# A 128-byte spare tile behind the constants' pool, and two steps of a two-layer hybrid decoder issued two ticks later

## The chip, the cores and the metric

One Trainium2 chip, one NeuronCore of it. The metric is the device time of one execution in microseconds (us), the median of three. Engines are named as in the profile: PE is TensorE (PEld its weight loads), DVE VectorE, ACT ScalarE, POOL GpSimd, SP SyncE.

## What is computed

Two layers of a decoder trunk on x of 512 tokens by 1024 channels, float32:

```python
for l in range(2):
    x = x + 0.5 * swiglu(rms_norm(x, ffn1_norm[l]), ffn1_w_up[l], ffn1_w_down[l])   # hidden 2816
    h = rms_norm(x, mix_norm[l])
    q, k, v, z, xbc, dt_raw, gate_sb, gate_ssm = split(h @ w_in[l])
    y_sb = stick_breaking_attention(q, k, v) @ w_branch_sb[l]                       # 4 heads of 128
    xbc = silu(causal_depthwise_conv(xbc, conv_w, conv_b))                          # 4 taps
    y_ssm = mamba2_ssd(z, xbc, dt_raw, ...) @ w_branch_ssm[l]                       # 24 heads of 64, 8 groups
    x = x + (sigmoid(gate_sb) * y_sb + sigmoid(gate_ssm) * y_ssm) @ w_out[l]
    x = x + 0.5 * swiglu(rms_norm(x, ffn2_norm[l]), ffn2_w_up[l], ffn2_w_down[l])
return rms_norm(x, final_norm)
```

## The kernel before

x is kept transposed, as 8 blocks of 128 channels by 512 tokens. Every large product is done at nearly fp32 precision with three fp32r matmuls, `mm3` (L313): high part by high part (L315 in the trace), high by low (L316) and low by high (L317). A weight unit (128x1024) is read from HBM into `wraw`, cast on ACT into `whi` (L282) and its remainder taken on DVE into `wlo` (L284, `convert`). Activations are split alike: `hhi`/`hlo` hold a normed or scaled block, `th`/`tl` differences of two half blocks, `act` the FFN's hidden blocks, `yt` the mixer's transposed tiles (q, k, later the SSM's output), `ohi`/`olo` the attention's output.

The FFN's up product works on 2x2 blocks with seven products in place of eight (`pair_of_blocks`, L576): matmuls of 256 columns, four of seven products with `th`/`tl` as the operand that streams and three with `hhi`/`hlo`. Most others stream 512 columns.

**Order of work.** The engines run what the program text issues, in order. After each `mm3` of a long product `dense` (L320) calls `tick()` (L208), which moves every side generator on whose count has run out; `yield n` in a generator means "go on n ticks later", so n ticks stand for n times three matmuls on PE. The generators that matter here:

- `norm_end` (L522): sums the squares of x over channels. ACT casts the sum `acc` to `rs` (L527), DVE takes the remainder `sq` (L529), PE sums both over the partitions with two matmuls by `nones` (L533), ACT computes an estimate of the reciprocal root (L537 to L539), DVE refines it (L541 to L543). It is spawned six times: at the opening, behind the first FFN of each layer (for the mixer's norm), behind each mixer, and behind the first layer's second FFN. In the FFN and the opening, products start on blocks that are not yet normed, and are scaled by `rs` afterwards; in the mixer the first three products do so, then DVE scales the eight blocks of x in place (`scale_blocks`, L363) and splits them again (`swapped`, L355), since the later products take normed blocks.
- `conv_block` (L1017): the four taps of the causal convolution on DVE (L1028, three instructions), tanh on ACT (L1033), the product that ends silu on DVE (L1040, into `cv`, `bT` or `cT`), then for the x and b blocks four (b: three) transposes on PE (`transposed`, L854) into a `pt` bank of PSUM, and a copy of them on ACT. x and b blocks of the 8 groups feed the groups' SSD steps.
- `mixer` (L1268) holds one loop that waits, while the program is being issued, until four blocks are scaled.

**Where tiles lie.** Pools that open on the left of SBUF follow one another from the pool of the constants, `cst`, on: constants, norm tiles, `hhi`/`hlo`, `wraw`, `whi`/`wlo`, `act`, the mixer's left pools. x, `uv`/`th`/`tl`, `yt` and `ohi`/`olo` are in pools on the right, laid out from the far end. In each partition the left tiles named here begin 96 bytes behind a multiple of 256, the right ones 224 behind one: left and right stand 128 bytes apart, counted within 256.

Of the kernel before, what the change touches and what calls it, by code (L numbers as in the profile page):

```python
# [8 lines left out]
F32 = mybir.dt.float32  # L9
# [8 lines left out]
P = 128  # L18
# [67 lines left out]
def conv_at(kind, i):  # L86

    if kind == "x":
        return OFF_X + i * P, i * TAPS
    at = (OFF_B, OFF_C)[kind == "c"] + i * P  # L90
    return at, (DIN // P + GROUPS * (kind == "c") + i) * TAPS
# [72 lines left out]
class Builder:  # L164
# [357 lines left out]
    def norm_end(self, wait):  # L522

        nc = self.nc
        yield wait - 2
        two = [self.t(self.nrm, [P, SEQ], tag, F32R) for tag in ("rs", "sq")]
        nc.scalar.copy(two[0], self.acc)  # L527
        yield 2
        nc.vector.tensor_tensor(two[1], self.acc, two[0].bitcast(F32), op=ALU.subtract)  # L529
        yield 2  # L530
        ps = self.t(self.ptr, [P, SEQ], "pt")
        for part in two:
            nc.tensor.matmul(ps, self.nones, part, start=part is two[0], stop=part is two[1])  # L533
        yield 3
        y, t = self.t(self.nrm, [P, SEQ], "rs"), self.t(self.nrm, [P, SEQ], "acc")
        v = self.t(self.nrm, [P, SEQ], "sq")
        nc.scalar.activation(y, ps, AF.Ln, scale=-1.0 / DM, bias=self.eps)  # L537
        nc.scalar.activation(y, y, AF.Exp, scale=-0.5)
        nc.scalar.activation(v, ps, AF.Identity, scale=-1.0 / DM, bias=self.eps)  # L539
        yield 3  # L540
        nc.vector.tensor_tensor(t, y, v, op=ALU.mult)  # L541
        nc.vector.scalar_tensor_tensor(t, t, -0.5, y, op0=ALU.mult, op1=ALU.mult)
        nc.vector.scalar_tensor_tensor(y, t, 1.5, y, op0=ALU.add, op1=ALU.mult)  # L543
        self.rs = y
# [472 lines left out]
    def conv_block(self, kind, i, ps):  # L1017


        nc, mp = self.nc, self.mp  # L1020
        r = yield from self.take("raw")
        u = yield from self.take("cv")
        _, k0 = conv_at(kind, i)
        tap = [self.conv[:, k0 + j:k0 + j + 1] for j in range(TAPS)]
        nc.scalar.activation(u, ps, AF.Identity, scale=tap[KCONV - 1], bias=tap[KCONV])
        yield 2
        for j in range(1, KCONV):
            nc.vector.scalar_tensor_tensor(u[:, j:], ps[:, :SEQ - j], tap[KCONV - 1 - j], u[:, j:],  # L1028
                                           op0=ALU.mult, op1=ALU.add)
            yield 1  # L1030
        yield 1
        yield from self.opened()
        nc.scalar.activation(r, u, AF.Tanh)  # L1033
        yield 1
        if self.cumb is None:
            self.load_cum(0)
        dst = u
        if kind != "x":
            dst = self.ssm[i][kind] = self.t(mp, [P, SEQ], kind + "T")
        nc.vector.scalar_tensor_tensor(dst, r, 1.0, u, op0=ALU.add, op1=ALU.mult)  # L1040
        yield 3
        if kind == "x":
            p, i = divmod(i, 3)
            pt = self.transposed(dst)
            yield 1
            for g in (2 * p, 2 * p + 1):
                a, b = max(i * P, g % 2 * GW), min((i + 1) * P, (g % 2 + 1) * GW)
                if a < b:
                    if "x" not in self.ssm[g]:
                        while not self.room["xs"]:  # L1050
                            yield 1
                        self.room["xs"] -= 1
                        self.ssm[g]["x"] = self.t(mp, [P, NT, GW], "xs", bufs=3)
                    nc.scalar.activation(self.ssm[g]["x"][:, :, a - g % 2 * GW:b - g % 2 * GW],
                                         pt[:, :, a - i * P:b - i * P], AF.Copy, scale=0.5)
                    self.ssm[g]["x", i] = True
            yield 1
        elif kind == "b":
            pt = self.transposed(dst, NT - 1)
            yield 1  # L1060
            tok = self.t(mp, [P, NT - 1, P], "btok")
            nc.scalar.copy(tok, pt)
            self.ssm[i]["btok"] = tok
        self.give("raw", "cv")
# [326 lines left out]
    def build(self):  # L1391
        nc, tc, enter = self.nc, self.tc, self.ctx.enter_context
        self.cst = enter(tc.tile_pool(name="cst", bufs=1))
        self.nrm = enter(tc.tile_pool(name="nrm", bufs=1))
        self.hp = enter(tc.tile_pool(name="hp", bufs=KB))
        self.wraw = enter(tc.tile_pool(name="wraw", bufs=3))
        self.wsp = enter(tc.tile_pool(name="wsp", bufs=3))
        self.dr = enter(tc.tile_pool(name="dr", bufs=2, space=DRAM))
        self.pmm = enter(tc.tile_pool(name="pmm", bufs=4, space=PSUM))
        self.pa = enter(tc.tile_pool(name="pa", bufs=2, space=PSUM))  # L1400
        self.ptr = enter(tc.tile_pool(name="ptr", bufs=2, space=PSUM))
        self.open_x()
        self.open_t()
        self.tt = [self.t(self.tp, [P, SEQ], "tl", bufs=KB) for _ in range(KB)]
        nc.scalar.preload_act_table_set("natural_log_exp_and_others")
        self.pars = [self.cst.tile([P, NPAR], F32, name=f"par{layer}") for layer in range(DEPTH)]
        self.opening_loads()
        self.consts()
        warm = self.t(self.ptr, [P, SEQ], "pt")
        for _ in range(8):  # L1410
            nc.tensor.matmul(warm[:, :P], self.ones, self.ones, start=True, stop=True)
        self.norm_start()
        for m in range(KB):
            self.spawn(self.norm_square(m), 16 + m)
        self.spawn(self.norm_end(30))
        for layer in range(DEPTH):
            par = self.pars[layer]
            self.ffn(layer, 1, par[:, G_FFN1:G_FFN1 + KB], par[:, G_MIX:G_MIX + KB])
            self.mixer(layer)
            if layer < DEPTH - 1:  # L1420
                self.ffn(layer, 2, par[:, G_FFN2:G_FFN2 + KB], self.pars[layer + 1][:, G_FFN1:G_FFN1 + KB])
        self.xg = [None] * KB
        self.ffn(DEPTH - 1, 2, self.pars[DEPTH - 1][:, G_FFN2:G_FFN2 + KB], None)
        self.close_t()
        self.xpool.__exit__(None, None, None)
# [107 lines left out]
```

## Time and profile before

| | |
|---|---|
| median of three runs | 2587.27 us (2586.95 to 2587.41) |
| the profiled execution | 2588.58 us, of it 2586.9 us from the first to the last instruction |
| PE busy | 2565.8 us, 99% of the span, 15028 matmuls |
| DVE, ACT, POOL busy | 1752.7 (68%), 1281.7 (50%), 499.3 us (19%) |
| granted TensorE clock | mean 0.999 of full speed |
| chain that ended last | PE 93%, DVE 4%, ACT 2% |

The profile gives busy shares over the whole span first and then the chain of work that ended last, followed back from the end. Waits of an engine are listed by line and by what ended them; the timeline gives each instruction's start and length. Matmuls are pipelined: one is listed as longer than the distance to the next one's start, so distances between starts are what PE's time is made of.

### The profile page before, as it was taken

To read this page: it belongs to the slowest core of one execution; us is meant where nothing else is said; L and a number is where in the kernel's file an instruction comes from. 1 tells how busy PE (TensorE), PEld (TensorE's weight loads), DVE (VectorE), ACT (ScalarE), POOL (GpSimd) and SP (SyncE) were. 2 spreads that over 40 slices of the span, in tenths; PEclk is the share of its full clock that TensorE was granted. 3 is DMA by queue.
4 is the path that set the end of the run, shared out by engine and by line. 5 is a ranking of instruction groups with operands and counts; after the bars stand their busy time and mean duration, and the time that the engine had idled before them with its cause. 6 is when DMAs were issued, how large, how long until landed. Compare 5 with 4: busy or idle time off the path is not lost.

```text
span 2586.9 us, 38169 instructions
## 1 busy us (share of the span) xinstructions
PE 2565.8 (99%) x15028; PEld 2289.6 (89%) x15028; DVE 1752.7 (68%) x2426; ACT 1281.7 (50%) x2103; POOL 499.3 (19%) x614
## 2 busy tenths in 40 slices
PE   9999999999999999999999999999999999999998
PEld 8898988888888889899998989888888888899997
DVE  8576875676664478586885858756666644776766
ACT  6343556655554255343653535566555533543444
POOL 0121201143341002121121312012433310022120
PEclk9999999999999999999999999999999999999999
DMA  6454442233333455545364544423333334456452
GB/s 188 132 157 138 131 138 87 99 103 110 103 107 105 132 161 140 167 139 162 108 180 139 155 143 136 136 74 109 98 106 107 111 112 135 153 141 172 140 163 78
DMA packets 104659, 335.76 MB, mean 130 GB/s; under 512 B 11872, under 2 KB 15392, under 8 KB 104480
## 3 DMA queue, kind: packets, MB, share of 16 engines
q1 hardware_dynamic: 92672, 292.84, 33.9%
q0 software_dynamic: 10944, 39.85, 8.6%
q8 instruction: 118, 1.93, 0.3%
q10 hardware_dynamic: 864, 0.64, 0.1%
q14 instruction: 61, 0.50, 0.1%
HBM read 320.60 MB, written 12.68 MB: 129 GB/s over the span
## 4 chain that ended last, share of the span: by engine, by line
PE 93%; DVE 4%; ACT 2%; issue 1%; DMA 0%; POOL 0%; DVEq 0%; SPq 0%; ACTq 0%
PE mm L315 26%; PE mm L317 25%; PE mm L316 25%; PE pa L316 3%; PE pa L317 3%; PE pa L315 3%; PE pa L1170 2%; DVE wlo L284 1%; PE pa L1172 1%; PE pt L854 1%; PE pt L1155 1%; DVE cv L1028 1%; PE pt L1153 1%; ACT whi L282 1%; PE pa L453 1%
## 5 line engine op out<-in xcount | busy, mean ns | idle before, releaser
L282 ACT CAST whi<-wraw 128x1024 fp32r<-128x1024 f32 (+3 forms) x440 | 434.8, 989 | 593.0 <-PE mm L317 492.5
L284 DVE TENSOR_TENSOR wlo<-wraw,whi 128x1024 fp32r<-128x1024 f32 (+3 forms) x440 | 538.9, 1225 | 168.8 <-ACT whi L282 167.3
L315 PE MATMUL mm<-hhi,whi 128*128 128x512 f32 (+1 forms) x1584 | 564.5, 356 | 0.0
L317 PE MATMUL mm<-hlo,whi 128*128 128x512 f32 (+1 forms) x1584 | 553.4, 349 | 0.4 <-DVE hlo L507 0.4
L316 PE MATMUL mm<-hhi,wlo 128*128 128x512 f32 (+1 forms) x1584 | 552.3, 349 | 0.0
L317 PEld LDWEIGHTS mm<-hlo,whi 128*128 128x128 f32 x1584 | 299.7, 189 | 40.4 <-DVE hlo L507 0.8
L316 PEld LDWEIGHTS mm<-hhi,wlo 128*128 128x128 f32 x1584 | 300.1, 189 | 34.4
L315 PEld LDWEIGHTS mm<-hhi,whi 128*128 128x128 f32 x1584 | 300.0, 189 | 34.4 <-ACT hhi L505 0.4
L284 DVE TENSOR_TENSOR wlo<-s,whi 128x1024 fp32r<-128x1024 f32 x152 | 235.2, 1562 | 60.3 <-ACT whi L282 60.3
L315 PE MATMUL mm<-act,whi 128*128 128x512 f32 (+1 forms) x710 | 273.9, 386 | 0.0
L317 PE MATMUL mm<-act,whi 128*128 128x512 f32 (+1 forms) x710 | 273.9, 386 | 0.0
L316 PE MATMUL mm<-act,wlo 128*128 128x512 f32 (+1 forms) x710 | 273.9, 386 | 0.0
L315 PE MATMUL mm<-th,whi 128*128 128x256 f32 x912 | 257.1, 282 | 0.0
L317 PE MATMUL mm<-tl,whi 128*128 128x256 f32 x912 | 256.7, 281 | 0.0
L316 PE MATMUL mm<-th,wlo 128*128 128x256 f32 x912 | 256.5, 281 | 0.0
L626 POOL TENSOR_TENSOR g<-g,rs 128x512 f32<-128x512 f32 x76 | 132.7, 1747 | 554.9 <-DVE g L633 536.0
L282 ACT CAST whi<-s 128x1024 fp32r<-128x1024 f32 x152 | 159.3, 1048 | 102.4 <-PE mm L317 60.7
L652 DVE SCALAR_TENSOR_TENSOR x<-mm,x 128x512 f32<-128x512 f32 x93 | 64.1, 689 | 196.0 <-PE mm L317 196.0
L254 POOL DMA_DIRECT2D s<-in_wflat_dram x76 | 65.8, 865 | 625.0 <-DMA s<-in_wflat_dram 331.3
L315 PEld LDWEIGHTS mm<-th,whi 128*128 128x128 f32 x912 | 172.1, 189 | 0.0
L316 PEld LDWEIGHTS mm<-th,wlo 128*128 128x128 f32 x912 | 171.8, 188 | 0.0
L317 PEld LDWEIGHTS mm<-tl,whi 128*128 128x128 f32 x912 | 171.7, 188 | 0.0
(306 smaller groups left out, 5094.6 us busy)
## 6 DMA issues: line engine op xcount, KB each, us to landing
wraw<-in_wflat_dram SPq DMA_DIRECT2D x328, 512.0 KB, 3.6
s<-in_wflat_dram SPq DMA_DIRECT2D x76, 512.0 KB, 4.6
s<-in_wflat_dram POOLq DMA_DIRECT2D x76, 512.0 KB, 7.4
wraw<-in_wflat_dram SPq DMA_DIRECT2D x88, 384.0 KB, 3.1
cumb<-cum_d SPq DMA_DIRECT2D x16, 768.0 KB, 4.8
xd<-x SPq DMA_DIRECT2D x16, 256.0 KB, 3.3
wraw<-in_wflat_dram SPq DMA_DIRECT2D x16, 256.0 KB, 3.3
x<-xd SPq DMA_DIRECT2D x16, 256.0 KB, 3.8
```

Of the source, the lines that this page charges most:

```text
L254: self.nc.gpsimd.dma_start(raw, src, accum_op=ALU.add)
L282: nc.scalar.copy(hi[:, :n], raw[:, :n])
L284: nc.vector.tensor_tensor(lo[:, :n], raw[:, :n], hi[:, :n].bitcast(F32), op=ALU.subtract)
L315: mm(ps, a[0], b[0], start=start, stop=False, **kw)
L316: mm(ps, a[1], b[0], start=False, stop=False, **kw)
L317: mm(ps, a[0], b[1], start=False, stop=stop, **kw)
L453: nc.tensor.matmul(p, parts[a][:, ks], h[b], start=k + a + b == 0, stop=k == KB - 1 and b == 1)
L626: eng.tensor_tensor(r, r, self.rs[:, cols].unsqueeze(1).to_broadcast([P, 2, half]), op=ALU.mult)
L652: self.nc.vector.scalar_tensor_tensor(x, pd, 0.5, x, op0=ALU.mult, op1=ALU.add)
L854: self.nc.tensor.transpose(pt[:, cs], src[:, cs], self.ident)
L1028: nc.vector.scalar_tensor_tensor(u[:, j:], ps[:, :SEQ - j], tap[KCONV - 1 - j], u[:, j:], op0=ALU.mult, op1=ALU.add)
L1170: nc.tensor.matmul(py[:, i * HD:(i + 1) * HD], decs[c][:, i, :], xdts[c][:, i, :], start=True, stop=True)
```

## The change

Three edits. `cst` gets a first tile of 32 fp32 per partition that nothing reads or writes: every left tile lies 128 bytes higher, right tiles stay. In `norm_end` the pair of matmuls and all that follows is issued two ticks later. In `conv_block` the transposes and the copies from them are issued two ticks later, and so is the return of the block's two tiles (`give`), which a later block takes.

```diff
@@ norm_end
         yield 2
         nc.vector.tensor_tensor(two[1], self.acc, two[0].bitcast(F32), op=ALU.subtract)
-        yield 2
+        yield 4
         ps = self.t(self.ptr, [P, SEQ], "pt")
@@ conv_block
         nc.vector.scalar_tensor_tensor(dst, r, 1.0, u, op0=ALU.add, op1=ALU.mult)
-        yield 3
+        yield 5
         if kind == "x":
@@ build
         self.cst = enter(tc.tile_pool(name="cst", bufs=1))
+        self.cst.tile([P, 32], F32, name="gap")
         self.nrm = enter(tc.tile_pool(name="nrm", bufs=1))
```

No instruction is added or removed on any engine. Tile names carry a running number, which the spare tile raises by one; lines behind L1394 stand one lower. Three places where the order of an engine moves:

DVE at the norm ahead of the first layer's mixer, before (`wlo` is a weight unit's low part, L541 to L543 refine the norm's root, L363 scales a block of x):

```order
L529 TENSOR_TENSOR sq_3480<-acc_3234,rs_3479 128x512
L284 TENSOR_TENSOR wlo_3489<-wraw_3403,whi_3488 128x1024
L541 TENSOR_TENSOR acc_3515<-rs_3514,sq_3516 128x512
L542 SCALAR_TENSOR_TENSOR acc_3515<-acc_3515,rs_3514 128x512
L543 SCALAR_TENSOR_TENSOR rs_3514<-acc_3515,rs_3514 128x512
L363 SCALAR_TENSOR_TENSOR x_86<-x_86,par_106,rs_3514 128x512
L363 SCALAR_TENSOR_TENSOR x_87<-x_87,par_106,rs_3514 128x512
L284 TENSOR_TENSOR wlo_3530<-wraw_3440,whi_3529 128x1024
```

The same place in the change:

```order
L529 TENSOR_TENSOR sq_3481<-acc_3235,rs_3480 128x512
L284 TENSOR_TENSOR wlo_3490<-wraw_3404,whi_3489 128x1024
L284 TENSOR_TENSOR wlo_3531<-wraw_3441,whi_3530 128x1024
L541 TENSOR_TENSOR acc_3525<-rs_3524,sq_3526 128x512
L542 SCALAR_TENSOR_TENSOR acc_3525<-acc_3525,rs_3524 128x512
L543 SCALAR_TENSOR_TENSOR rs_3524<-acc_3525,rs_3524 128x512
L363 SCALAR_TENSOR_TENSOR x_87<-x_87,par_107,rs_3524 128x512
```

The second weight remainder (`wlo_3530`, now `wlo_3531`) stands ahead of the norm's three instructions instead of behind them and two blocks of L363. On ACT the cast that feeds it stays behind L539, the last of the norm's three activations.

PE in the mixer's SSD part, first layer, one of the convolved x blocks, before (`cv` is the convolved block, `pt` the bank that takes its transposes, `raw` a group's result, which another generator transposes):

```order
L317 MATMUL mm_5907<-hlo_3589,whi_5799 128x512
L854 MATMUL pt_5925<-ident,cv_5853 128x128 x4
L315 MATMUL mm_5907<-hhi_3596,whi_5799 128x512
L316 MATMUL mm_5907<-hhi_3596,wlo_5800 128x512
L317 MATMUL mm_5907<-hlo_3597,whi_5799 128x512
L854 MATMUL pa_5935<-ident,raw_5893 128x128 x4
```

and in the change:

```order
L317 MATMUL mm_5908<-hlo_3589,whi_5792 128x512
L315 MATMUL mm_5908<-hhi_3597,whi_5792 128x512
L316 MATMUL mm_5908<-hhi_3597,wlo_5793 128x512
L317 MATMUL mm_5908<-hlo_3598,whi_5792 128x512
L315 MATMUL mm_5908<-hhi_3604,whi_5792 128x512
L316 MATMUL mm_5908<-hhi_3604,wlo_5793 128x512
L317 MATMUL mm_5908<-hlo_3605,whi_5792 128x512
L854 MATMUL pt_5935<-ident,cv_5852 128x128 x4
L315 MATMUL mm_5908<-hhi_3611,whi_5792 128x512
L316 MATMUL mm_5908<-hhi_3611,wlo_5793 128x512
L317 MATMUL mm_5908<-hlo_3612,whi_5792 128x512
L854 MATMUL pa_5944<-ident,raw_5901 128x128 x4
```

The transposes stand six matmuls of 512 columns later, and so does the work of the group around them.

DVE ahead of the transposes of the second convolved x block of the layer (`z` is the gate of the SSM), before:

```order
L1028 SCALAR_TENSOR_TENSOR cv_4819<-mm_4717,conv_4132,cv_4819 128x509
L1087 SCALAR_TENSOR_TENSOR z_4382<-raw_4853,z_4382 128x384
L1028 SCALAR_TENSOR_TENSOR cv_4857<-mm_4774,conv_4132,cv_4857 128x511
L284 TENSOR_TENSOR wlo_4860<-wraw_4718,whi_4859 128x1024
L1040 SCALAR_TENSOR_TENSOR cv_4819<-raw_4818,cv_4819 128x512
```

and in the change:

```order
L1028 SCALAR_TENSOR_TENSOR cv_4828<-mm_4718,conv_4133,cv_4828 128x509
L1028 SCALAR_TENSOR_TENSOR cv_4847<-mm_4775,conv_4133,cv_4847 128x511
L284 TENSOR_TENSOR wlo_4850<-wraw_4719,whi_4849 128x1024
L1087 SCALAR_TENSOR_TENSOR z_4370<-raw_4863,z_4370 128x384
L1028 SCALAR_TENSOR_TENSOR cv_4847<-mm_4775,conv_4133,cv_4847 128x510
L1087 SCALAR_TENSOR_TENSOR z_4383<-raw_4872,z_4383 128x384
L1028 SCALAR_TENSOR_TENSOR cv_4847<-mm_4775,conv_4133,cv_4847 128x509
L1040 SCALAR_TENSOR_TENSOR cv_4828<-raw_4827,cv_4828 128x512
```

Here PE reaches the transposes 12 matmuls later, and on DVE four more instructions (two L1087, two L1028) stand between the weight remainder and L1040.

## Rows read from the trace of the kernel before

**Rows 1.** The page: busy time of each engine, its share and instructions.

```profile
PE 2565.8 (99%) x15028; PEld 2289.6 (89%) x15028; DVE 1752.7 (68%) x2426; ACT 1281.7 (50%) x2103; POOL 499.3 (19%) x614
```

**Rows 2.** Waits of PE, by line and releaser: us in total, times, longest us.

```profile
PE pt L854 <- DVE cv L1040: 4.8, 8, 0.8
...
PE pt L533 <- DVE sq L529: 0.7, 1, 0.7
```

**Rows 3.** Timeline of PE, one site of transposes: start, us, instruction [idle before, releaser].

```profile
608.49 0.39 PE L317 MATMUL mm<-hlo,whi 128*128 128x512 f32 x1
609.41 0.66 PE L854 MATMUL pt<-ident,cv 128*128 128x128 f32 x4 [0.54 <-DVE cv L1040]
```

**Rows 4.** Timeline of DVE at the same site.

```profile
608.67 0.69 DVE L1040 SCALAR_TENSOR_TENSOR cv<-raw,cv 128x512 f32<-128x512 f32 x1 [0.16 <-ACT raw L1033]
```

**Rows 5.** Timeline of PE, the first late site of the layer.

```profile
507.35 0.39 PE L317 MATMUL mm<-hlo,whi 128*128 128x512 f32 x1
508.50 0.33 PE L854 MATMUL pt<-ident,cv 128*128 128x128 f32 x1 [0.76 <-DVE cv L1040]
```

**Rows 6.** Timeline of DVE at the first late site.

```profile
505.96 0.74 DVE L1028 SCALAR_TENSOR_TENSOR cv<-mm,conv,cv 128x511 f32<-128x511 f32 x1
506.62 1.21 DVE L284 TENSOR_TENSOR wlo<-wraw,whi 128x1024 fp32r<-128x1024 f32 x1
507.76 0.68 DVE L1040 SCALAR_TENSOR_TENSOR cv<-raw,cv 128x512 f32<-128x512 f32 x1
```

**Rows 7.** Timeline of PE, the norm behind the first layer's second FFN.

```profile
1300.07 0.39 PE L533 MATMUL pt<-rs,nones 128*128 128x512 f32 x1
1301.17 0.50 PE L533 MATMUL pt<-sq,nones 128*128 128x512 f32 x1 [0.72 <-DVE sq L529]
```

**Rows 8.** Timeline of DVE from the mixer's norm to the first tiles of q and k.

```profile
364.24 0.69 DVE L541 TENSOR_TENSOR acc<-rs,sq 128x512 f32<-128x512 f32 x1 [2.83 <-ACT sq L539]
...
367.82 1.22 DVE L284 TENSOR_TENSOR wlo<-wraw,whi 128x1024 fp32r<-128x1024 f32 x1
368.95 3.40 DVE L363 SCALAR_TENSOR_TENSOR x<-x,par,rs 128x512 f32<-128x512 f32 x5
...
381.81 1.88 DVE L408 TENSOR_TENSOR yt<-raw,yt 128x512 fp32r<-128x512 f32 x3
```

**Rows 9.** Timeline of ACT and of PE, the same stretch.

```profile
364.99 1.06 ACT L282 CAST whi<-wraw 128x1024 fp32r<-128x1024 f32 x1 [0.79 <-PE pa L317]
...
383.15 0.33 PE L316 MATMUL pa<-yt,yt 128*128 128x128 f32 x1 [0.45 <-DVE yt L408]
```

**Rows 10.** Timeline of PE, ends of runs of equal matmuls of 512 columns: `act`, then `yt`.

```profile
99.21 0.39 PE L316 MATMUL mm<-act,wlo 128*128 128x512 f32 x1
...
105.11 0.39 PE L315 MATMUL mm<-act,whi 128*128 128x512 f32 x1
...
834.56 0.39 PE L315 MATMUL mm<-yt,whi 128*128 128x512 f32 x1
...
840.86 0.40 PE L315 MATMUL mm<-ohi,whi 128*128 128x512 f32 x1
```

**Rows 11.** Timeline of PE, starts of runs of 256 columns: `th`, `hhi`, `th`, `hhi`, `th`.

```profile
999.63 0.28 PE L315 MATMUL pa<-th,whi 128*128 128x256 f32 x1
...
1005.33 0.28 PE L315 MATMUL pa<-hhi,whi 128*128 128x256 f32 x1
...
1008.19 0.28 PE L315 MATMUL mm<-th,whi 128*128 128x256 f32 x1
...
1011.04 0.28 PE L315 MATMUL mm<-hhi,whi 128*128 128x256 f32 x1
...
1016.80 0.28 PE L315 MATMUL mm<-th,whi 128*128 128x256 f32 x1
```

**Rows 12.** Groups of PE instructions by line and shape: count | busy us, mean ns.

```profile
L315 PE MATMUL mm<-th,whi 128*128 128x256 f32 x912 | 257.1, 282 | 0.0
...
L315 PE MATMUL mm<-yt,whi 128*128 128x512 f32 x192 | 75.8, 395 | 0.0
```

## The prediction

> **What bounds the kernel.** I read the busy times first: PE is busy for 99% of the span, with DVE next at 68% [rows 1]. Only two things can move the end, then: the few places where PE waits, and the distance from one matmul's start to the next one's. The list of PE's waits comes second, for the places that the two later yields aim at: the transposes of convolved blocks wait for L1040 on DVE 8 times, 4.8 us together, and the norm's pair waits for L529 once, 0.7 us [rows 2]. Third come the timelines around these places, where a stall is read as the distance between two starts less the usual one, and last the runs of equal matmuls, since the spare tile adds no work and can act through addresses alone. All durations are from the profiled execution; it took 2588.58 us, 1.31 more than the median of 2587.27, and I take the sum of differences off the median. 0.2% of it, about what a measurement can tell from no change, is 5.2 us.
>
> **Transposes two ticks later.** In a run of 512 columns, 26 matmuls take 105.11 - 99.21 = 5.90 us, 0.227 each [rows 10]. At one site the next start comes after 609.41 - 608.49 = 0.92 us [rows 3], so the stall is 0.69; its wait is listed as 0.54. The first late site of a layer has 508.50 - 507.35 = 1.15, a stall of 0.92, listed as 0.76 [rows 5]. 2 x 0.76 + 6 x 0.54 = 4.8, which is the list's total: two sites are of the second kind (one in each layer), six of the first. Together they cost 6 x 0.69 + 2 x 0.92 = 6.0 us.
>
> At the six sites the changed order puts six matmuls ahead, 1.36 us. PE would come to the transposes at 608.49 + 0.23 + 1.36 = 610.08; L1040 starts at 608.67 and runs 0.69, to 609.36 [rows 4]. On DVE it keeps its predecessors there, merely in another sequence, so 0.7 us are to spare and the stall goes: **-4.1 us**.
>
> At the two first sites PE comes 12 matmuls later, at 507.35 + 0.23 + 12 x 0.227 = 510.30, but L1040 moves too: two L1087 and two L1028 now stand between the weight remainder and it. The remainder holds DVE until 507.76, where L1040 starts now [rows 6]; an L1028 holds it for 506.62 - 505.96 = 0.66 us, and with four times that at most, L1040 starts by 510.4 and ends by 511.1 with its 0.68. That is up to 0.8 us behind PE, beside a stall of 0.92 now. I take **0** for the two, with -1.8 (both gone) and +0.6 as ends, the latter if the L1087 are held up by their own inputs.
>
> What else goes with the block: its copies on ACT and the return of its buffers come 1.4 us later, and ten of the sixteen group steps move with them, as a whole, so what a group's matmuls wait for keeps its distance from them. SP issues one load of `cumb` in each layer behind a weight load instead of ahead of it, and POOL takes six sums of y one place later. PE lists no wait for any of that work beside L854, so I cost it at nothing; the cover is the ready time of operands off PE, and if a few sites lose it, each costs what a site costs now, 0.7 us. Three such are the upper end, +2.
>
> **Norm sums two ticks later.** The one norm that waits now has 1301.17 - 1300.07 = 1.10 us between the matmuls of its pair [rows 7], 0.87 over the usual. 1.36 us later `sq` is long there: **-0.9 us**. Everything behind the pair is later too, in all six norms. Behind four of them (opening, FFNs) PE goes on with products that are scaled by `rs` afterwards, and only full PSUM banks could stop it; PE lists no wait for them, and I take 0, with +1 as an end.
>
> The other two lead to the mixer, and there PE does wait for what the norm releases: the first product of q and k waits 0.45 us at 383.15 for a `yt` that DVE makes at 381.81 to 383.69 [rows 8, 9]. Between 364.24, where L541 begins, and there DVE goes from one instruction to the next, so a delay of L541 arrives in full. How large is it? L541 starts when ACT's L539 is done, now at about 364.2. In the changed order L539 ends 1.36 later, at 365.6, and next on ACT stands the cast of a weight, 1.06 us long, to 366.6 [rows 9]. Its remainder on DVE stands **ahead** of L541 now: it holds DVE from 366.6 for 368.95 - 367.82 = 1.13 us [rows 8], so L541 starts at 367.7, 3.5 us later than now. The remainder is then missing from the queue behind, which gives 1.13 back. The `yt` come 2.4 us later, and PE with them: **+4.8 us** for the two layers. The lower end is the shift of the ticks alone, 2 x 1.36 = +2.7; the upper one 2 x 2.9, if the remainder's place is not given back in full.
>
> **The spare tile.** Nothing uses it; left tiles move from 96 to 224 bytes past a multiple of 256, where the right ones stand already. So I compared runs of equal matmuls by where their operands lie. With 512 columns and both on the left, the step is 0.2269 us; with `yt` on the right and weights on the left it is (840.86 - 834.56) / 27 = 0.2333 [rows 10]. 192 such matmuls on each of three lines [rows 12] and, by the widths in the reference (512 beside 1536), a third as many for the attention's output: 768 x 6.4 ns = 4.9 us that equal remainders may save. With 256 columns it is the other way about: `th` on the right takes (1005.33 - 999.63) / 48 = 118.75 ns, and (1011.04 - 1008.19) / 24 the same; `hhi` on the left takes 2.86 + 5.76 us for 72 of them, 119.7 [rows 11]. 912 on each of three lines into `mm` [rows 12], and a third of that into `pa` (one product in four), are 3648 with `th`; they may lose 0.97 ns each, 3.5 us. The ends are -4.9 and +3.5. I take both effects, **-1.4 us**, since in either width the step goes with the two operands' distance, and the change sets all pairs to the distance at which both of the other classes were seen.
>
> The Trainium skill, page "SBUF — State Buffer", section "SBUF: two separate sides", says that PE's own ports never wait on another engine, and it names no cost for where within a partition an operand begins. By it the spare tile would be worth 0; the two steps of rows 10 differ by 3%, which that does not explain, though the rows cannot tell the distance of the operands from the side on which one of them lies.
>
> **Sum:** -4.1 - 0.9 + 4.8 - 1.4 = -1.6 us, so 2587.27 - 1.6 = **2585.7 us**.
>
> **Rivals.**
> - *Slower: DVE, not the tick, sets the transposes.* At the first site the order already shows L1040 sliding back behind other work. If it slides at all eight sites by as much as PE's 1.36 us, the 4.1 us stay and the norms' +4.8 stand alone: -0.9 + 4.8 - 1.4 = +2.5, 2589.8 us; with three new stalls of 0.7 beside it, 2591.9. It decides at 610.08: an L1040 that ends more than 0.7 us later than now. For it: the first sites. Against it: at the six others its predecessors are the same. Chance 0.14.
> - *Faster: 512 columns gain and 256 do not lose.* The 1 ns could come from the order of the products or their PSUM banks rather than from addresses; the 6.4 ns is too large for that. Then -4.1 - 0.9 + 4.8 - 4.9 = -5.1, 2582.2 us; if the mixer's norm also costs only its two ticks, 2580.1. Chance 0.27.
> - *The addresses do nothing.* The side of SBUF, or `yt` itself, makes the step; moving left tiles then changes none. -4.1 - 0.9 + 4.8 = -0.2, 2587.1 us. Chance 0.19. The rule of the Trainium skill's page "SBUF — State Buffer" above would give this time too.
> - *The mixer's norm costs less.* If ACT takes the weight's cast before it has finished the norm's three activations, or DVE's queue has slack that the timeline hides, +2.7 in place of +4.8: 2583.6 us. Chance 0.12.
>
> The forecast itself has 0.28.
>
> **Range and chances.** All the cases but their joint ends lie within 2580.0 (addresses gain, mixer cheap) and 2591.0 (transposes' stall stays): that is the range. Faster by over 0.2% needs less than 2582.1: half of the second rival, and a little of the last, 0.22. Slower by over 0.2% needs more than 2592.4: the far end of the first rival, 0.08. The rest, 0.70, is within 0.2%.
>
> **What would show it.** In the changed profile: the list of PE's waits has L854 twice (one in each layer, some 0.4 to 0.8 us) and no L533; the first product of q and k waits some 2.5 us longer, for `yt`, with L541 at about 367.7 and a weight remainder just ahead of it; `yt` by weights steps at 0.227, `th` at 0.1197. The prediction is wrong if L854 is still there eight times, if `yt` at the mixer's start comes within a microsecond of its old time, or if the steps do not move.

## The result and the profile after

| | before | after |
|---|---|---|
| median of 20 runs | 2587.12 us (2586.58 to 2588.68) | 2590.32 us (2589.84 to 2592.2) |
| ratio | | 1.0014, 95% interval 1.0007 to 1.002 |
| profiled execution, its span | 2588.58, 2586.9 us | 2590.39, 2588.7 us |

The change costs 3.2 us, where the forecast (2585.7) was a gain of 1.6. That is within 0.2% and inside the forecast's range, but clear of the interval of the measurement and to the other side. Busy times say nothing, as before:

The page of the changed kernel, head line and busy times.

```profile
span 2588.7 us, 38186 instructions
...
PE 2565.6 (99%) x15028; PEld 2295.2 (89%) x15028; DVE 1752.5 (68%) x2426; ACT 1280.8 (49%) x2103; POOL 481.7 (19%) x614
```

The list of PE's waits does, against [rows 2] (us in total, times, longest):

```profile
PE pa L316 <- DVE yt L408: 3.7, 2, 1.9
PE pt L1153 <- DVE state L1163: 2.1, 2, 1.1
PE pt L854 <- DVE cv L1040: 1.6, 2, 0.8
...
PE mm L317 <- DVE hlo L355: 1.0, 2, 0.5
```

L854 waits twice instead of eight times, and the norm's pair (L533) is gone from the list, as forecast. `yt` is waited for longer, as forecast. L1153 is **new**: a matmul of the SSD steps that waits for a PSUM bank. So is L317's wait for `hlo`, ahead of q and k. The forecast had neither row.

**Where the time went.** Both kernels issue the same 13878 matmuls on L315 to L317. The n-th of them is looked up in either trace, and the difference of its start is followed through the program:

| stretch (us of the trace before) | after less before |
|---|---|
| opening, to 71 us | -1.4 |
| FFN up products: 71 to 346, 921 to 1265, 1317 to 1610, 2185 to 2574 | +4.9 |
| mixers' norm to q and k: 346 to 399, 1610 to 1717 | +3.8 and +2.3 |
| attention and SSD: 399 to 813, 1717 to 2073 | -0.9 and -1.0 |
| merge, out: 813 to 921, 2073 to 2185 | -2.5 and -2.4 |
| norm behind the second FFN: 1265 to 1317 | -1.0 |
| sum | +1.8 |

The opening is not of the change. Its first matmuls, before:

```profile
6.58 1.05 PE L453 MATMUL pa<-hhi,wlo 128*128 128x512 f32 x2
7.43 1.05 PE L453 MATMUL pa<-hlo,whi 128*128 128x512 f32 x2
...
18.63 0.39 PE L315 MATMUL mm<-hhi,whi 128*128 128x512 f32 x1
```

and after:

```profile
6.85 0.62 PE L453 MATMUL pa<-hlo,whi 128*128 128x512 f32 x2
7.40 0.73 PE L453 MATMUL pa<-hhi,whi 128*128 128x512 f32 x2
...
17.20 0.39 PE L315 MATMUL mm<-hhi,whi 128*128 128x512 f32 x1
```

Two matmuls take 0.85 us in the one, 0.55 in the other, and the first L315 starts 1.4 us apart. In the ten other traces of this study the first L315 starts between 16.9 and 17.2 us or between 18.3 and 18.7, whatever the edit. The execution of before that the rows came from happened to be one with the long opening: that accounts for the 1.31 us by which it exceeded the median. The three others with a long opening exceed their own medians too, by 1.0 to 1.6 us. Without the opening the two traces differ by 1.8 + 1.4 = **+3.2 us**, which is the difference of the medians.

**Transposes**, the site of [rows 3, 4] in the changed kernel: PE, then DVE.

```profile
614.58 0.39 PE L317 MATMUL mm<-hlo,whi 128*128 128x512 f32 x1
614.81 0.60 PE L854 MATMUL pt<-ident,cv 128*128 128x128 f32 x4
...
613.33 0.69 DVE L1040 SCALAR_TENSOR_TENSOR cv<-raw,cv 128x512 f32<-128x512 f32 x1
```

The step is 0.23 now where it was 0.92, and L1040 ends at 614.02, 0.8 us ahead. At the first late site ([rows 5, 6]) the stall moved along with PE, 1.22 us between starts where it was 1.15:

```profile
513.48 0.39 PE L317 MATMUL mm<-hlo,whi 128*128 128x512 f32 x1
514.70 0.66 PE L854 MATMUL pt<-ident,cv 128*128 128x128 f32 x4 [0.83 <-DVE cv L1040]
```

**The new wait**, 40 us behind it: PE, then DVE.

```profile
552.80 0.40 PE L317 MATMUL mm<-hlo,whi 128*128 128x512 f32 x1
554.27 0.46 PE L1153 MATMUL pt<-cT,bT 128*128 128x128 f32 x2 [1.07 <-DVE state L1163]
...
550.99 0.75 DVE L1028 SCALAR_TENSOR_TENSOR cv<-mm,conv,cv 128x511 f32<-128x511 f32 x1 [1.41 <-ACT cv L1025]
551.93 1.46 DVE L284 TENSOR_TENSOR wlo<-wraw,whi 128x1024 fp32r<-128x1024 f32 x1 [0.19 <-ACT whi L282]
553.31 0.54 DVE L1161 TENSOR_TENSOR dec<-pt,dec 128x384 f32<-128x384 f32 x1
553.78 0.34 DVE L1163 COPY state<-pt 128x192 f32<-128x192 f32 x1
```

L1161 and L1163 read the bank that the next chunk step writes. They stand behind the first tap of the *next* conv block, which waits 1.41 us for ACT, and a weight remainder behind that. Before, the same pair stood ahead of both:

```profile
543.20 0.55 DVE L1161 TENSOR_TENSOR dec<-pt,dec 128x384 f32<-128x384 f32 x1
543.66 0.35 DVE L1163 COPY state<-pt 128x192 f32<-128x192 f32 x1
...
546.02 0.75 DVE L1028 SCALAR_TENSOR_TENSOR cv<-mm,conv,cv 128x511 f32<-128x511 f32 x1
546.95 1.23 DVE L284 TENSOR_TENSOR wlo<-wraw,whi 128x1024 fp32r<-128x1024 f32 x1 [0.18 <-ACT whi L282]
```

The distance between two starts on PE is 554.27 - 552.80 = 1.47 us in the change; less the usual 0.23, that is 1.24 us a layer.

**The mixer's norm**, against [rows 8, 9]: DVE, then PE.

```profile
366.14 1.23 DVE L284 TENSOR_TENSOR wlo<-wraw,whi 128x1024 fp32r<-128x1024 f32 x1 [5.12 <-ACT whi L282]
367.28 0.69 DVE L541 TENSOR_TENSOR acc<-rs,sq 128x512 f32<-128x512 f32 x1
...
378.45 0.50 PE L317 MATMUL mm<-hlo,whi 128*128 128x512 f32 x1 [0.52 <-DVE hlo L355]
...
382.91 0.22 PE L315 MATMUL pa<-yt,yt 128*128 128x128 f32 x1
384.99 0.33 PE L316 MATMUL pa<-yt,yt 128*128 128x128 f32 x1 [1.86 <-DVE yt L408]
385.27 0.69 PE L315 MATMUL mm<-hhi,whi 128*128 128x512 f32 x1
385.76 0.63 PE L316 MATMUL mm<-hhi,wlo 128*128 128x512 f32 x1
386.18 0.63 PE L317 MATMUL mm<-hlo,whi 128*128 128x512 f32 x1
```

The remainder is ahead of L541, which starts at 367.28; this trace is 0.4 us ahead of the other's there, so that is the forecast 367.7. The wait for `yt` grew to 2.08 us between starts (382.91 to 384.99); before, the matmul ahead of it started 0.67 us before the 383.15 of [rows 9]:

```profile
382.48 0.22 PE L315 MATMUL pa<-yt,yt 128*128 128x128 f32 x1
```

Another 0.8 us is lost ahead of it, in and just behind the wait for `hlo`. What comes behind the wait for `yt` was not forecast: matmuls of 512 columns take 0.42 us each. The windows of that stretch, and of the second layer's, give the reason (each row: busy us of each engine, then the granted clock, DMA share and GB/s):

```profile
384.00:386.00 2.00, 1.01 (x4) 0.92 (x5) 2.00 (x4) 0.00 (x0) 0.00 (x0) 0.83 0.57 119
386.00:388.00 2.00, 2.00 (x7) 1.71 (x7) 1.31 (x3) 1.82 (x3) 0.00 (x0) 0.50 0.35 143
388.00:390.00 2.00, 2.00 (x9) 1.56 (x9) 1.55 (x3) 1.87 (x7) 0.18 (x1) 0.82 0.01 4
390.00:392.00 2.00, 2.00 (x10) 1.69 (x9) 1.05 (x3) 1.30 (x4) 0.40 (x2) 1.00 0.68 182
...
1668.00:1670.00 2.00, 1.24 (x7) 1.09 (x8) 1.91 (x4) 0.05 (x1) 0.00 (x0) 1.00 0.70 233
```

The granted clock fell to 0.50, the lower of its two levels (1.2 GHz), behind a wait of 2.1 us, and stayed there for some 3 us. Behind the second layer's wait, 2.10 us long, it did not. That is the difference between the two mixers, 3.8 and 2.3 us.

**Steps by address**, against [rows 10, 11]: `yt` by weights, then `th`.

```profile
834.61 0.39 PE L315 MATMUL mm<-yt,whi 128*128 128x512 f32 x1
...
842.77 0.39 PE L315 MATMUL mm<-ohi,whi 128*128 128x512 f32 x1
...
999.86 0.28 PE L315 MATMUL pa<-th,whi 128*128 128x256 f32 x1
...
1005.62 0.28 PE L315 MATMUL pa<-hhi,whi 128*128 128x256 f32 x1
```

36 steps in 8.16 us are 0.2267 each (0.2333 before); 48 steps in 5.76 us are 0.1200 each (0.1188 before). Both moved the way that was forecast.

### The profile page after: what moved, and what is told of

Its sections match the earlier page's. It is cut to its first block, busy times and chain, and to the rows that moved or that the text cites. A ratio compares the mean times of both kernels' runs of the same rounds, so it can differ in the third digit from the quotient of the medians.

```text
span 2588.7 us, 38186 instructions
## 1 busy us (share of the span) xinstructions
PE 2565.6 (99%) x15028; PEld 2295.2 (89%) x15028; DVE 1752.5 (68%) x2426; ACT 1280.8 (49%) x2103; POOL 481.7 (19%) x614
## 4 chain that ended last, share of the span: by engine, by line
PE 94%; DVE 4%; ACT 2%; issue 1%; DMA 0%; POOL 0%; DVEq 0%; SPq 0%; ACTq 0%
PE mm L315 26%; PE mm L317 26%; PE mm L316 26%; PE pa L316 3%; PE pa L317 3%; PE pa L315 3%; PE pa L1170 2%; DVE wlo L284 1%; PE pa L1172 1%; PE pt L1155 1%; PE pt L854 1%; PE pt L1153 1%; PE pa L453 0%; ACT whi L282 0%; DVE cv L1028 0%
## 5 line engine op out<-in xcount | busy, mean ns | idle before, releaser
L315 PE MATMUL mm<-hhi,whi 128*128 128x512 f32 (+1 forms) x1584 | 566.0, 357 | 0.0
L317 PE MATMUL mm<-hlo,whi 128*128 128x512 f32 (+1 forms) x1584 | 554.1, 350 | 1.4 <-DVE hlo L355 1.0
L316 PE MATMUL mm<-hhi,wlo 128*128 128x512 f32 (+1 forms) x1584 | 553.0, 349 | 0.0
L317 PEld LDWEIGHTS mm<-hlo,whi 128*128 128x128 f32 x1584 | 300.1, 189 | 42.3 <-DVE hlo L355 1.9
L316 PEld LDWEIGHTS mm<-hhi,wlo 128*128 128x128 f32 x1584 | 300.7, 190 | 34.1
L315 PEld LDWEIGHTS mm<-hhi,whi 128*128 128x128 f32 x1584 | 300.6, 190 | 34.1 <-ACT hhi L505 0.4
L315 PE MATMUL mm<-act,whi 128*128 128x512 f32 (+1 forms) x710 | 274.0, 386 | 0.0
L316 PE MATMUL mm<-act,wlo 128*128 128x512 f32 (+1 forms) x710 | 273.8, 386 | 0.0
L317 PE MATMUL mm<-act,whi 128*128 128x512 f32 (+1 forms) x710 | 273.6, 385 | 0.0
L315 PE MATMUL mm<-th,whi 128*128 128x256 f32 x912 | 258.1, 283 | 0.0
L316 PE MATMUL mm<-th,wlo 128*128 128x256 f32 x912 | 258.1, 283 | 0.0
L317 PE MATMUL mm<-tl,whi 128*128 128x256 f32 x912 | 258.1, 283 | 0.0
L315 PEld LDWEIGHTS mm<-th,whi 128*128 128x128 f32 x912 | 175.1, 192 | 0.0
L316 PEld LDWEIGHTS mm<-th,wlo 128*128 128x128 f32 x912 | 175.1, 192 | 0.0
L317 PEld LDWEIGHTS mm<-tl,whi 128*128 128x128 f32 x912 | 175.1, 192 | 0.0
```

The lines of the kernel that those rows point to most:

```text
L315: mm(ps, a[0], b[0], start=start, stop=False, **kw)
L316: mm(ps, a[1], b[0], start=False, stop=False, **kw)
L317: mm(ps, a[0], b[1], start=False, stop=stop, **kw)
```

## The experiments

Each is an edit of the kernel before, unless it is said otherwise; the theories are those of the expectation above each result. "By the trace" is the difference of starts as in the table above, counted from 72 us on, so that the opening is left out.

**The spare tile alone.**

```diff
+        self.cst.tile([P, 32], F32, name="gap")
```

> Only the spare tile. Theory A (distance counted within 256 bytes sets the step, in both widths): yt by weights 0.2269 us, th by weights 0.1200 us, PE's list of waits as before; -4.9 us and +5.2 us, together +0.4 us against before. Theory B (the later yields moved the steps, not the tile): steps stay 0.2333 and 0.1188, 0 us. Theory C (the spare tile costs in the waits too): the list of waits has a new entry and the sum is above +1.5 us.

Measured 2587.5 us against 2587.05, ratio 1.0002 (0.9994 to 1.0011); by the trace +0.1. The FFN stretches lose 4.9 us, the merge stretches gain 4.8, and the waits are those of before. Theory A. The tile's two effects are real and cancel.

**A second spare tile, in the pool of `th`.**

```diff
+        self.cst.tile([P, 32], F32, name="gap")
...
+        self.tp.tile([P, 32], F32, name="side", bufs=1)
```

> The spare tile, and a second one of 128 bytes ahead of th, tl and uv on the right, so that these stand 128 bytes from the weights again while yt and ohi do not. Theory A (distance): th by weights back at 0.1188 us, yt at 0.2269 us: -4.5 us against before. Theory B (the absolute place of the weights, not the distance): th stays at 0.1200, +0.4 us.

2587.09 us against 2587.05, ratio 1.0 (0.9991 to 1.0008); `th` at 0.1200. That reads like theory B, but it says nothing about either: in that pool the tile came to lie behind the others, and `th` and `tl` kept their addresses. It is the first experiment over again. The next one puts it where it moves them.

**A pool of its own for the second tile.**

```diff
     def open_t(self):
 
+        self.sidepool = self.tc.tile_pool(name=self.name("side"), bufs=1, side="right")
+        self.sidepool.__enter__().tile([P, 32], F32, name=self.name("spare"))
...
+        self.cst.tile([P, 32], F32, name="gap")
```

> The spare tile, and a pool of one more 128-byte tile on the right ahead of the pool of th, tl and uv, so that these now do stand 128 bytes from the weights, counted within 256, while yt and ohi stand at the same remainder. Theory A (distance): th by weights back at 0.1188 us, yt at 0.2269: some -4.5 us against before. Theory B (where the weights lie, not the distance): th stays at 0.1200, 0 us.

2582.23 us against 2587.15, ratio 0.9982 (0.9973 to 0.999); by the trace -4.9. A run of `th` in it:

```profile
997.23 0.28 PE L315 MATMUL pa<-th,whi 128*128 128x256 f32 x1
...
1002.92 0.28 PE L315 MATMUL pa<-hhi,whi 128*128 128x256 f32 x1
```

5.69 us for 48 steps, 0.1185: only `th`'s place differs from the first experiment, and the step of 256 columns is back, while the merge keeps its gain. Theory A: for these operands the distance counts, and it counts in opposite ways at 512 and 256 columns. At 512 columns no run moves `yt` away from the moved weights again; there the reading rests on `act`, which lies with the weights in both kernels and steps at 0.227 in both.

**The norm's yield alone.**

```diff
-        yield 2
+        yield 4
         ps = self.t(self.ptr, [P, SEQ], "pt")
```

> Only the norm's yield of 4. Theory A (ticks and the weight remainder ahead of L541 both delay the mixer's first products): the wait of L316 for yt grows by 1.4 us in each layer, with a new wait of 0.7 us for hlo ahead of it and 0.3 behind: +2.35 us a layer, less 1.0 for the norm that waited: +3.7 us. Theory B (only the ticks, the remainder is given back at once): +1.36 a layer, +1.7 us.

2592.02 us against 2587.05, ratio 1.0019 (1.001 to 1.0027); by the trace +5.0, of which 1.5 is a stretch at half clock behind the first layer's wait. Without it +3.5: theory A. Its eleven executions stand in three groups some 1.5 us apart (2590.5 to 2591.0, 2591.9 to 2592.2, 2593.2 to 2593.8), as an opening of either length and a clock that falls behind a mixer's wait or does not would put them.

**The pair later, what follows it not.**

```diff
-        yield 2
+        yield 4
...
-        yield 3
+        yield 1
         y, t = self.t(self.nrm, [P, SEQ], "rs"), self.t(self.nrm, [P, SEQ], "acc")
```

> The norm's pair two ticks later, but what follows it is issued where it was (the yields are 4 and 1), so that the weight remainder stays behind L541. Theory A: only 1.36 us of delay is left: L541 at 365.6, the wait for yt 1.36 longer in each layer, less 1.0: +1.7 us. Theory B (the remainder's place is worth nothing): as with the norm's yield alone, within 0.5 us of it. Theory C (DVE has slack behind L541): -1.0 us.

2590.32 us against 2587.05, ratio 1.0013 (1.0004 to 1.0022). By the trace +1.36 in the first mixer and +2.9 in the second, -1.0 at the norm. There the clock fell behind the second layer's wait (windows, columns as above):

```profile
1666.00:1668.00 2.00, 2.00 (x8) 1.64 (x8) 1.31 (x3) 1.79 (x3) 0.00 (x0) 0.50 0.24 96
```

Without that the sum is +1.7, theory A: with the weight remainder behind L541 the delay is the ticks alone, 1.36 us; the remainder's place is worth another 1.0 us a layer.

The eleven executions show the clock apart from the wait. Three took 2588.4 to 2588.5 us at a mean granted clock of 0.999, four 2590.2 to 2590.4 at 0.998, three 2591.7 to 2591.9 at 0.997 and one 2593.3 at 0.997. The traced one is of the second group and has one fall, so no, one and two falls are the likely reading of the first three groups, which stand 1.5 to 1.8 us apart. The first group, without a fall, is 1.4 us above before.

**The norm earlier ahead of the mixers.**

```diff
-        yield 2
+        yield 4 if self.xd is None else 1
         ps = self.t(self.ptr, [P, SEQ], "pt")
```

> The norm's yield is 1 ahead of the mixers and 4 elsewhere. Theory A (what releases the mixer's first products is a chain from the norm's pair on, without slack): L541 0.7 us earlier, the wait of L316 for yt (0.6 us between starts) gone in both layers, the L533 wait behind the second FFN gone: -1.0 - 1.2 = -2.2 us, and no fall of the granted clock behind the wait. Theory B (another operand is as late): -1.0 us.

2585.09 us against 2587.15, ratio 0.9991 (0.9982 to 1); by the trace -2.0: -0.5 in each mixer, -1.0 at the norm. Neither L316 nor L533 waits. Theory A: the chain from the pair to `yt` has no slack in either direction.

**The conv block's yield alone.**

```diff
-        yield 3
+        yield 5
         if kind == "x":
```

> Only the conv block's yield of 5. Theory A (six stalls of L854 go, the two first sites stay, and the first chunk step of a group, which slides behind the next block's L1028 and a weight remainder on DVE, gives its PSUM bank back late): L854 waits 2 times, L1153 waits 2 times for some 1.2 us each; -4.1 + 2.5 + 0.6 = -1.0 us. Theory B (the wait of L1153 comes from the norm's shift or the spare tile): no L1153 in the list, -3.5 us or less.

2584.57 us against 2587.15, ratio 0.999 (0.9981 to 0.9999); by the trace -2.6. Its list of waits holds the rows that were named:

```profile
PE pt L1153 <- DVE state L1163: 2.1, 2, 1.1
PE pt L854 <- DVE cv L1040: 1.7, 2, 0.8
```

So L1153's wait comes from this edit and from nothing else: theory A, though the gain is 1.6 us larger than expected. -4.2 for the six sites, +2.5 for L1153 and +0.1 for the two first sites are in the trace. Another -0.7 is in the merge, where `yt` by weights steps at 0.2324 on the mean in place of 0.2333, with operands at the same distance within 256 bytes; so the distance is not all that sets this step, and what else does stays open. The last 0.4 were not traced to a cause.

**x blocks only.**

```diff
-        yield 3
+        yield 5 if kind == "x" else 3
         if kind == "x":
```

> The yield of 5 for the x blocks only, b blocks keep 3. In this order the group's first L1161 and L1163 stand ahead of the next block's L1028 and the weight remainder again. Theory A (the place behind those two on DVE makes the wait of L1153): L1153 leaves the list, L854 waits twice at most; -4.1 us, and up to 1 us more if the first sites gain too. Theory B (the transposes of a b block take the second PSUM bank between two chunk steps, which is so in both orders): L1153 still waits 1.2 us twice, -1.7 us.

2579.87 us against 2587.15, ratio 0.9971 (0.996 to 0.9982); by the trace -7.3. The list of waits begins with what stood behind them:

```profile
PE pa L967 <- DVE y L408: 1.6, 6, 0.5
PE pt L1411 <- DVE ones L469: 1.1, 1, 1.1
PE pa L316 <- DVE yt L408: 0.9, 2, 0.5
```

Neither L1153 nor L854 waits any more. Theory A: a b block's transposes still take the second bank between two chunk steps, so that is not the cause; what changed is the place of L1161 and L1163 on DVE, ahead of the next block's tap and the weight remainder again:

```profile
543.92 0.35 DVE L1163 COPY state<-pt 128x192 f32<-128x192 f32 x1
544.95 0.75 DVE L1028 SCALAR_TENSOR_TENSOR cv<-mm,conv,cv 128x511 f32<-128x511 f32 x1 [0.68 <-ACT cv L1025]
545.88 1.22 DVE L284 TENSOR_TENSOR wlo<-wraw,whi 128x1024 fp32r<-128x1024 f32 x1 [0.18 <-ACT whi L282]
```

The two first sites, which were expected to keep most of their stall, gained too: here L1040 stays ahead of the next block's taps there. The gain is 2 us and more above what was expected: the eight stalls are 6.0 of it and the merge 0.7, as in the last experiment; 0.6 were not traced to a cause.

**The change with the mixers' norm put back.**

```diff
-        yield 4
+        yield 4 if self.xd is None else 2
         ps = self.t(self.ptr, [P, SEQ], "pt")
```

(this one against the changed kernel)

> The change, but ahead of the two mixers the norm's yield is 2 again. Theory A (what made the change slower is the mixers' wait for yt, 2.1 us between starts in place of 0.7, its 0.9 us of smaller waits beside it, and a granted clock that falls behind the long wait in some places): against the change -2 x 2.3 - 1.45 = -6.0 us, 2584.3 us, 2.8 below before, and no stretch at half clock behind 383 and 1667 us. Theory B (the norm's shift costs elsewhere too, or the clock falls for another reason): above 2586.

2583.99 us against 2587.23, ratio 0.9988 (0.9979 to 0.9997), 6.3 us below the changed kernel's 2590.32. The granted clock is 1.00 in every window of 2 us from 382 to 392 and from 1664 to 1674 us. Theory A. Added to this 2584.0, the mixers' 2 x 2.3 us give an estimate of 2588.6 for the changed kernel without a fall of the clock. All twenty of its executions lie at 2589.8 or above, so its median most likely has one fall in it, as its trace has.

**What gained, together**: the two spare tiles, the norm at 1 ahead of the mixers and 4 elsewhere, the conv block at 5 for x blocks.

> The parts that gained, together: the spare tile with the second one on the right, the norm's yield 1 ahead of the mixers and 4 elsewhere, the conv block's yield of 5 for x blocks alone. Theory A (the parts add up: -4.9, -2.1, -7.3 us): 2587.1 - 14.3 = 2572.8 us. Theory B (a gain in one place is lost to the next bound, DVE in the SSD part above all): above 2575.

2573.1 us against 2587.23, ratio 0.9945 (0.9931 to 0.9959): 14.1 us less than before. Theory A: the parts add up.

## Why the prediction was wrong

The forecast was -1.6 us and the measurement +3.2. Three terms made the difference: a wait that was costed at nothing (+2.5 us), the granted clock (+1.5) and the loss at 256 columns (+1.4). The first alone turns the forecast's gain into a loss.

- *Transposes.* Right. Six stalls went (-4.2), and the two first sites kept theirs (0.98 us in place of 0.92).
- *Norm behind the second FFN.* Right: -1.0, forecast -0.9.
- *Mixer's norm.* The mechanism and the chain were right: +2.3 us a layer, forecast +2.4, though only 1.4 of it is in the wait for `yt`, where all was expected. **What was not in the sum is the clock:** a wait of 2.1 us on PE lets the granted clock fall to half in some places, 1.5 us more in the first layer of the trace. The forecast read the waits as times that PE loses once.
- *The spare tile.* Both effects have the sign that was forecast, -4.9 at 512 columns as worked out. **The loss at 256 columns was mis-sized**, +4.9 for +3.5: `th` rose by 1.25 ns to 0.1200, not to the 0.1197 of `hhi`, and `hhi` itself rose by a quarter of a nanosecond, 0.7 us over 2736 steps. The distance does not explain that last part: `hhi` and the weights move together, and with the second spare tile, which moves `th` alone, `hhi` is back at its old step.
- *"What else goes with the block ... I cost it at nothing."* **This step failed.** The group steps move "as a whole", so their operands keep their distance; but DVE's queue is shared with the conv blocks and the weight remainders, which do not move with them. The pair that frees the PSUM bank slid behind two of these: +2.5 us. The edit of the conv block alone shows this wait, and it goes with the pair's place on DVE. The range held such stalls (three sites of 0.7, +2), the sum did not.

The sum: -1.6 + 2.5 + 1.5 + 1.4 = +3.8, with 0.6 us of small differences the other way, half of them in the SSD part, against +3.2 measured. None of the rivals was the case: the one that ended slower put the loss at the transposes, by L1040 sliding at all eight sites, which it did only at the first of each layer. That its 2589.8 us lies close to the measured 2590.3 is chance: the stalls at the six sites went, and other losses took their place. That the time stayed inside the forecast's range says as little for the sum.

The rule of the Trainium skill, page "SBUF — State Buffer", section "SBUF: two separate sides", that PE waits on nobody at its SBUF ports, gives no step that depends on where an operand begins. The first spare tile moved the step by 2.8% at 512 columns and 1% at 256, with nothing else changed; here the measurement decides.

## What to carry to other kernels

When a step is issued later, look at each engine it shares, not only at the distances inside the step: what it overtakes or falls behind on the busiest helper decides which buffer comes free late. A wait of the bounding engine that grows can cost more than its length, by the granted clock behind it: here PE's wait went from 0.7 to 2.1 us, and in three of the six places traced the clock behind it cost some 1.5 us more. Read the windows' clock there as well as the wait. A yield that helps at one place need not help at all that share the code: here the two yields split by place gained 7.3 and 2.1 us, where one number for all gained 2.6 and lost 5.0.

## What was not expected of the hardware

- Behind a wait of 2.1 us the granted clock fell to 0.50 for some 3 us in the first layer of one execution, and not in the second layer with the same wait; in another kernel, with waits of 2.0 us, it fell in the second and not in the first. In the nine traces where these waits were 0.7 us or none, the clock's entries show no fall before the last matmuls. The Trainium skill, page "TensorE: Matmul & The Clock Gate", section "HAM oscillation — how this bites in real kernels", says that gaps in PE's work throw its clock back and the work behind pays. The rows agree that it can, though the page's example is of longer waits, for DMA; here half of the waits of 2.0 to 2.1 us traced had a fall behind them (three of six), so the length of the wait alone does not decide it.
- At the opening, steps of 512 columns took 0.427 us until 10.0 us in the execution of before and until 6.3 in the one of the change, and the first L315 came 1.4 us apart. 0.427 is the step at half clock above. The windows list 1.00 there, but the traces hold no entry of the clock so early: the first entry, at full clock, comes at 9.9 us before and at 6.4 in the change. In the twelve traces the first L315 starts at 18.3 us or later where that entry comes at 9.4 or later (four traces), and at 17.2 or earlier where it comes at 7.1 or earlier (eight). So the two lengths of the opening are most likely the clock too, rising later in some executions.
- Operands that begin 128 bytes apart, counted within 256, cost 6.4 ns a step at 512 columns and save 1.25 ns at 256 columns in this kernel. Why the sign turns was not tried.
